# Second-layer softmax without its normalising pass: reciprocal row sums carried as rows through DRAM into the head outputs

## The chip, the cores and the metric

The kernel runs on one core of one Trainium2 chip. The metric is device microseconds of that core for one execution of the whole program; less is better. The core has TensorE (PE in the profile; its weight loads are listed apart as PEld), VectorE (DVE), ScalarE (ACT), GpSimd (POOL) and SyncE (SP), which here issues nearly all DMAs. On-chip memory is SBUF (128 partitions); TensorE writes into PSUM banks.

## The reference, cut to what matters

Two transformer-like layers work on 512 latent and 256 context tokens of width 1024. Layer 0 mixes by differential attention, layer 1 by grouped-query attention: 8 query heads of 128, two key/value heads, keys and values over all 768 tokens. In the last layer only the 512 latent tokens are queries. The change lies in layer 1:

```python
s = jnp.einsum('bqhgd,bkhd->bhgqk', qblk.astype(jnp.float32), k32) * scale
p = jax.nn.softmax(s, axis=-1)
return jnp.einsum('bhgqk,bkhd->bqhgd', p.astype(v.dtype), v)
...
def attend(qq, kk, vv, gate):
    o = sweep_attention(qq, kk, vv)
    o = o.reshape(o.shape[0], o.shape[1], BRANCH_WIDTH)
    return (o * jax.nn.silu(gate)) @ w_out
...
x = x + gate * rms_norm(y, post_g[i])
```

A softmax row is exp(s - max) divided by its sum. The division is linear in the row, so it can be done on the probabilities (768 numbers for each query and head) or on the head's output (128 numbers).

## The kernel before

**Precision.** Each large product is done with operands split into a high and a low part (`hi`, `lo`, type fp32r): three matmuls stand for one (`mm3`, `pv_mm`). So a weight that comes in as `raw` is copied by ACT into `whi`, and the remainder is taken into `wlo` by POOL or DVE.

**One head of layer 1.** Tokens are worked in four blocks of 128 queries (`m` = 0 to 3); two blocks make a pair (`ch` = 0, 1), so there are 8 x 2 = 16 pairs. For one block, `s1_units` does this: PE computes the scores of 128 queries by 768 keys into a two-bank PSUM tile (`sc`); DVE finds the negated row maximum; ACT takes the exponential into one half of an SBUF tile `pp` and sums each row into a small tile `l`; DVE inverts the sum; POOL multiplies the block by it in place (`scaled`, with `EN1 = 'p'`). After the second block of the pair, `turn` transposes the whole `pp` (128 x 1536) on DVE in blocks of 32 x 32, stores it to DRAM (`dr<-pp`, 768 KB) and loads it back in four pieces (`at<-dr`, 192 KB each), so that keys lie on the partitions. Two `pp` tiles and two `at` tiles are in turn.

`pv1_steps` then works on the pair in three steps of 256 keys: ACT copies a piece of `at` into `ah`, DVE takes the remainder into `al`, and PE multiplies both by the values into a bank of 256 columns. The output is transposed: features on partitions, the 256 queries of the pair along the row. ACT copies it into the head's tile `gT1[h]` (`g` in the profile). When both pairs of a head are done and its gate `sz` (SiLU of a projection) is there, POOL multiplies the head by the gate (`gate_mul1`); for the last head DVE does it half by half (`last_half`). All heads are split once more (`h<-g`) and enter the output projection, whose first quarter runs over seven heads while the last head is unfinished.

Beside this, PE has the projections of q and of the gate z to do, which a generator queue hands out as filling work. The q projection is followed by its norm (ACT `jk`, POOL `qrs`), the rotary products (DVE `ta`, `tb`) and their sum (POOL `q`).

**Layer 0** has the same shape, with two softmaxes a head; its normalisation is not touched. During layer 0, twelve 1 MB tiles of the conditioning weights are loaded (`araw<-in_ada_g`) and multiplied on PE (`bk<-araw,s`).

**What sets the order.** The program is written twice: a first pass (`Plan`) records every instruction with what it must wait for; `price` gives each an estimated cost, `schedule` lists them by engine queue with a model of hand-over times, DMA landing and the slowing of DVE and POOL by each other (`op.kind`), and `shift` moves the sort keys of some groups of instructions at random, one seed of `MOVES` after the other. The queues' order that comes out is then fixed for all five engines. So a changed instruction, a changed price or a changed list of seeds can re-sort every queue, in layer 0 too. DRAM scratch tiles are handed out in a ring (`dram`), six of them (`DRB`).

The prices for DMAs, by size in bytes, as (bytes per ns, base ns):

```python
rate, base = {196608: (207, 1450), 786432: (420, 900), 131072: (350, 2500)}.get(op.cost, (350, 1450))
```

Of the kernel before, what the change touches and what calls it, by code (L numbers as in the profile page):

```python
# [9 lines left out]
F32 = mybir.dt.float32  # L10
F32R = mybir.dt.float32r
AF = mybir.ActivationFunctionType
ALU = mybir.AluOpType
# [3 lines left out]
P = 128  # L17
# [60 lines left out]
QTR = 2.0  # L78
EG0 = 'v'
EP0 = 'p'  # L80
EN1 = 'p'
ESW = 'v'
EG1 = 'a'
LM = (4.5, 4.5)
AB = 2
P0B = 2
# [1 line left out]
PPB = 2  # L88
DRSPLIT = 1
DRB = 6  # L90
PEWAY = ((), ())


def f32(ap):
# [29 lines left out]
SLACK = 0  # L124


# [15 lines left out]
def free_size(ap):  # L142
    n = 1
    for d in ap.shape[1:]:
        n *= d
    return n


class Plan:


    def __init__(self, mem, psum, drams, sizes):
        self.mem, self.drams, self.sizes, self.turns = mem, drams, sizes, 0
        self.psum = dict(psum)
        self.banks = {t.tensor.name: t.free_size() for t in psum.values()}
        self.width = mem.shape[1]
        self.ops, self.offs, self.tail, self.seen = [], [0], None, {}
        self.marks = []
        self.pools, self.stack = [], {"left": [], "right": []}
        for q in QUEUE:  # L160
            setattr(self, q, Queue(self.add, QUEUE[q]))
# [3 lines left out]
        return Pool(self, name, side, psum)  # L165

    def scratch(self):
        self.tile = lambda *args, **kw: self.dram()
        return nullcontext(self)

    def dram(self):
        self.turns += 1
        return self.drams[(self.turns - 1) % len(self.drams)]


    @contextmanager
# [39 lines left out]
    def add(self, q, meth, args, kw):  # L216
        op = Op()
        op.n, op.eng, op.meth, op.args, op.kw = len(self.ops), q, meth, args, kw
        op.prio = op.n - self.offs[-1]
        op.next, op.head = None, op  # L220
        self.ops.append(op)
        if self.sizes is None:
            return op
        aps = [a for a in args if isinstance(a, bass.AP)]
        outs, ins = aps[:1], aps[1:]
        for k, v in kw.items():
            if isinstance(v, bass.AP):
                (outs if k in ("out", "accum_out") else ins).append(v)
        op.preds, op.soft = set(), set()
        fresh = []  # L230
        for aps_, w in ((ins, 0), (outs, 1)):
            for ap in aps_:
                far = ap.space == bass.MemoryType.DRAM
                if far and all(ap.tensor.name != d.tensor.name for d in self.drams):
                    continue
                name, spans, parts = (ap.tensor.name, [(0, 2048)], 1) if far else self.places(ap)
                if name not in self.banks and not far:
                    at = spans[0][0]
                    p = next(p for p in self.pools if p.open and p.base <= at < p.base + p.size)
                    p.users.add(op)  # L240
                    if p.mark is not None:
                        op.preds.add(p.mark)
                    held = p.held[max(lo for lo in p.held if lo <= at)]
                    ring = held[0]
                    held[2].add(op)
                    op.preds |= held[3]
                    if held[1] is None:
                        held[1] = len(ring)
                        ring.append(op)
                    if held[1] and ring[held[1] - 1] is not op:  # L250
                        op.soft.add(ring[held[1] - 1])
                if w and q == "PE":
                    spans = [(0, self.banks[name] * 4)]
                for lo, hi in spans:
                    for pg in self.pages(name, lo, hi):
                        keep = []
                        for h in self.seen.get((name, pg), ()):
                            hop, hlo, hhi, hp, hw = h
                            meet = hlo < hi and lo < hhi and hp & parts
                            if hop is not op and ((w or hw) and meet or name in self.banks and hop.eng != q):  # L260
                                op.preds.add(hop)
                            elif hop is not op and name in self.banks:
                                op.soft.add(hop)
                            if meet and w and (lo <= hlo and hi >= hhi or name not in self.banks and lo <= max(hlo, pg * 2048) and hi >= min(hhi, pg * 2048 + 2048)) and not hp & ~parts:
                                continue
                            keep.append(h)
                        self.seen[name, pg] = keep
                    fresh.append((name, lo, hi, parts, w))
        for name, lo, hi, parts, w in fresh:
            for pg in self.pages(name, lo, hi):  # L270
                self.seen.setdefault((name, pg), []).append((op, lo, hi, parts, w))
        self.price(op, outs, ins)
        if self.tail is not None:
            op.head = self.tail.head
            self.tail.next = op
            op.soft.add(self.tail)
            op.head.preds |= {p for p in op.preds if p.head is not op.head}
            op.head.soft |= {p for p in op.soft if p.head is not op.head}
        return op
# [11 lines left out]
    def price(self, op, outs, ins):  # L291
# [47 lines left out]
                op.cost = 190 + 2.155 * n  # L339
        if q in ("DVE", "POOL") and op.kind is None and op.meth not in ("reciprocal", "tensor_reduce", "memset"):  # L340
            if not any(ps) and outs[0].tensor.name not in self.banks:
                op.kind = 0.75 if n <= 8 else 0.5 if sum(free_size(a) > 8 for a in ins) >= 2 else 0.25


    def schedule(self, rank):
# [15 lines left out]
        while len(order) < count:  # L361
# [28 lines left out]
            elif op.kind == "D":  # L390
                s = max(s, land.pop(0))
                go = s + (450 if op.cost == 131072 else 480 if op.cost == 196608 else 440)
                rate, base = {196608: (207, 1450), 786432: (420, 900), 131072: (350, 2500)}.get(op.cost, (350, 1450))
                dma = max(dma, go + 300) + op.cost / rate
                end = dma + base - 300 + DPAD
                land.append(end)
# [199 lines left out]
def tile_backbone(  # L596
# [33 lines left out]
    drp = ctx.enter_context(pl.scratch())  # L630

    def small(n=1):
        return sm.tile([P, 8], F32, tag="sm", name=nm("sm"), bufs=24)[:, :n]

    banks = [ps1.tile([P, 512], F32, tag=f"bk{i}", name=f"bk{i}", bufs=1) for i in range(4)]
    scs = [ps1.tile([P, 2, 512], F32, tag=f"sc{i}", name=f"sc{i}", bufs=1) for i in range(2)]
# [43 lines left out]
    def turn(pool, pp, w=384):  # L680
        flat = pp.rearrange("p b u x -> p (b u x)")
        nc.vector.transpose(flat, flat)
        at = pool.tile([P, 4, w], F32, tag=f"at{w}", name=nm("at"), bufs=ATB if w == 384 else 1)
        for lo in range(0, 4, 4 // DRSPLIT):
            n = 4 // DRSPLIT
            dr = drp.tile([P // DRSPLIT, 4 * 384], F32, tag="dr", name=nm("dr"), bufs=DRB)[:, :4 * w]
            nc.sync.dma_start(dr, flat[32 * lo:32 * (lo + n), :])
            for a in range(4):
                nc.sync.dma_start(
                    at[32 * a:32 * a + 32, lo:lo + n, :],  # L690
                    dr.rearrange("(q j) (a c) -> a j q c", j=32, c=w)[a])
        return at

    def dma_way(layer, h, ch):
        return (h, ch) not in PEWAY[layer]
# [1221 lines left out]
    with pl.pool("t1", "right") as t1p:  # L1917
        gT1 = [None] * KT
        ropeb = con.tile([P, 2, 512], F32, tag="rope", name="ropeb")
        nc.scalar.dma_start(ropeb, rope_b)  # L1920
        gq = t1p.tile([P, 2, P], F32, name="gq")
        nc.scalar.dma_start(gq, b_qk_g.partition_broadcast(P))
        cosb = ropeb[:, 0, :].rearrange("p (t d) -> p t d", t=4)
        sinb = ropeb[:, 1, :].rearrange("p (t d) -> p t d", t=4)
# [19 lines left out]
        def head_rstd(o, isk=True):  # L1944
            ssq = small(2)
            for j in range(2):
                jk = t1p.tile([P, P], F32, tag="jk", name=nm("jk"), bufs=1)
                nc.scalar.activation(jk, o[:, j * P:(j + 1) * P], AF.Square, accum_out=ssq[:, j:j + 1])
            r = t1p.tile([P, 2], F32, tag="qrs", name=nm("qrs"), bufs=16)
            if isk:  # L1950
# [106 lines left out]
        def z1_proj(h):  # L2057
# [13 lines left out]
            szt1[h] = sz  # L2071
            gate_mul1(h)

        def s1_units(h, ms):
            res, pair = [], {}
            moved = dma_way(1, h, ms[0] // 2)

            def unit(m):
# [20 lines left out]
                else:  # L2099
                    pt = unit_row(pair[0], m % 2)  # L2100
                    pv_, src = pt.rearrange("p (j n) -> p j n", j=2), scv
                l = small()
                nc.scalar.activation(pv_, src, AF.Exp, scale=sr, bias=nmx, accum_out=l)
                nc.vector.reciprocal(l, l)
                scaled(EN1, pt, pt, l)
                if not moved:
                    res.append(pt)
                elif m % 2:
                    res.append(turn(t1q, pair[0]))

            return res, [Step(lambda m=m: unit(m), 0.97) for m in ms]

        def pv1_steps(h, at, ch, after, ts, ms):
# [19 lines left out]
            def mstep(kt):  # L2133
# [6 lines left out]
                if kt == 4:  # L2140
                    if ch == 0:
                        gT1[h] = t1p.tile([P, 512], F32, tag="g1", name=nm("g1"), bufs=8)
                    (nc.scalar.copy if EG1 == "a" else nc.vector.tensor_copy)(*heads_out(gT1[h][:, ch * 256:ch * 256 + 256], o, moved))
                    close(o)
                    if ch == 1 and h < KT - 1:
                        done1.add(h)
# [234 lines left out]
```

## Time and profile before

| | |
|---|---|
| time, median of 3 runs | 755.72 us (755.34 to 755.8) |
| profiled execution, its own time | 757.93 us |
| its span, first to last instruction | 755.8 us |
| mean granted TensorE clock | 0.996 |
| DMA moved | 131.75 MB, mean 174 GB/s |

The span in 40 equal slices, in tenths of busy time (the last line is the granted clock):

```profile
PE   7999999999999999899999999999999989999996
PEld 6788888888878898797989998899999988888986
DVE  4445899988988869787889844789547787799744
ACT  6544477767676646666569853784476776678741
POOL 5463787885795738747755412467779887674201
PEclk9999999999999999999999999999999999999999
```

One slice is 18.9 us. Layer 0 runs to about 500 us, the projections of layer 1 follow, its attention lies between about 550 and 700 us, and the output projection runs to the end. In rows of groups and tiles, `a<-b,c` means that an instruction writes tile a from b and c; then come the shape, the count, the busy time and the mean of one, and the idle time of the engine just ahead of it with what ended it. In rows of order in time, the first two numbers are the start and the duration in us, and the bracket is the idle time ahead of the instruction and who ended it. A line of waits reads: who waited, on whom, us in total, times, longest.

### The profile page before, as it was taken

To read this page: it belongs to the slowest core of one execution; us is meant where nothing else is said; L and a number is where in the kernel's file an instruction comes from. 1 tells how busy PE (TensorE), PEld (TensorE's weight loads), DVE (VectorE), ACT (ScalarE), POOL (GpSimd) and SP (SyncE) were. 2 spreads that over 40 slices of the span, in tenths; PEclk is the share of its full clock that TensorE was granted. 3 is DMA by queue.
4 is the path that set the end of the run, shared out by engine and by line. 5 is a ranking of instruction groups with operands and counts; after the bars stand their busy time and mean duration, and the time that the engine had idled before them with its cause. 6 is when DMAs were issued, how large, how long until landed. Compare 5 with 4: busy or idle time off the path is not lost. (4 is left out here: it accounts for less than half of the span.)

```text
span 755.8 us, 13984 instructions
## 1 busy us (share of the span) xinstructions
PE 733.9 (97%) x5046; PEld 654.3 (87%) x5046; DVE 567.1 (75%) x881; ACT 480.0 (64%) x1085; POOL 466.7 (62%) x512
## 2 busy tenths in 40 slices
PE   7999999999999999899999999999999989999996
PEld 6788888888878898797989998899999988888986
DVE  4445899988988869787889844789547787799744
ACT  6544477767676646666569853784476776678741
POOL 5463787885795738747755412467779887674201
PEclk9999999999999999999999999999999999999999
DMA  9933263647474655835666182034436785888613
GB/s 347 405 123 124 95 198 109 188 164 223 140 221 142 212 165 176 255 100 172 229 171 179 31 307 84 2 97 157 145 117 190 224 257 163 232 239 266 165 46 111
DMA packets 51444, 131.75 MB, mean 174 GB/s; under 512 B 6448, under 2 KB 27184, under 8 KB 49840
## 3 DMA queue, kind: packets, MB, share of 16 engines
q1 hardware_dynamic: 47952, 125.73, 52.7%
q10 hardware_dynamic: 3424, 5.15, 2.1%
q8 instruction: 39, 0.64, 0.4%
q14 instruction: 29, 0.24, 0.1%
HBM read 97.56 MB, written 29.10 MB: 168 GB/s over the span
## 5 line engine op out<-in xcount | busy, mean ns | idle before, releaser
L509 PE MATMUL bk<-whi,h 128*128 128x256 f32 (+1 forms) x1184 | 244.0, 298 | 2.9 <-DVE tb L509 1.8
L509 PE MATMUL bk<-h,whi 128*128 128x512 f32 (+2 forms) x832 | 222.4, 348 | 0.1
L509 POOL TENSOR_TENSOR wlo<-raw,whi 128x256 fp32r<-128x256 f32 x200 | 171.1, 879 | 56.1 <-ACT whi L509 53.7
L509 PEld LDWEIGHTS bk<-whi,h 128*128 128x128 f32 x1184 | 189.6, 189 | 13.9 <-issue 2.9
L509 PE MATMUL bk<-wlo,h 128*128 128x256 f32 (+1 forms) x592 | 172.3, 298 | 0.0
L509 PEld LDWEIGHTS bk<-h,whi 128*128 128x128 f32 x832 | 144.4, 188 | 15.6 <-issue 2.8
L509 PE MATMUL bk<-h,wlo 128*128 128x512 f32 (+2 forms) x416 | 144.0, 348 | 0.0
L509 POOL TENSOR_SCALAR pp<-pp,sm 128x768 f32<-128x768 f32 (+1 forms) x78 | 82.0, 1054 | 68.0 <-DVE sm L509 58.4
L509 PEld LDWEIGHTS bk<-wlo,h 128*128 128x128 f32 x592 | 109.8, 188 | 4.9 <-issue 1.6
L509 DVE TENSOR_REDUCE sm<-sc 128x1 f32<-128x768 f32 (+2 forms) x114 | 101.0, 893 | 14.7 <-PE sc L509 14.5
L509 DVE TENSOR_TENSOR al<-at,ah 128x512 fp32r<-128x512 f32 x103 | 98.7, 978 | 13.7 <-ACT ah L509 9.9
L509 ACT CAST whi<-raw 128x1024 fp32r<-128x1024 f32 (+1 forms) x70 | 71.5, 1023 | 27.1 <-PE bk L509 14.9
L509 PEld LDWEIGHTS bk<-h,wlo 128*128 128x128 f32 x416 | 78.3, 188 | 8.7 <-issue 2.4
L509 ACT CAST ah<-at 128x512 fp32r<-128x512 f32 x103 | 61.7, 618 | 33.3 <-PE bk L509 21.0
L509 DVE STREAM_TRANSPOSE pp<-pp 128x1536 f32<-128x1536 f32 (+1 forms) x39 | 61.4, 1577 | 5.7 <-POOL pp L509 5.6
L509 DVE SCALAR_TENSOR_TENSOR pp<-p,sm,pp 128x768 f32<-128x768 f32 (+1 forms) x46 | 55.8, 1219 | 4.4 <-POOL pp L509 2.8
L509 PE MATMUL sc<-qk,qk 64*128 64x384 f32 (+1 forms) x480 | 50.7, 341 | 0.4 <-DVE qk L509 0.4
L509 ACT ACTIVATE jk<-bk 128x128 f32<-128x128 f32 (+4 forms) x66 | 22.7, 345 | 41.8 <-PE bk L509 22.8
L509 ACT ACTIVATE pp<-sc,sm 128x768 f32<-128x768 f32 (+1 forms) x46 | 35.4, 770 | 21.5 <-DVE sm L509 20.8
L509 PEld LDWEIGHTS sc<-qk,qk 64*128 64x128 f32 x480 | 38.3, 184 | 10.7 <-issue 3.5
L509 POOL TENSOR_TENSOR sz<-sz,za 128x384 f32<-128x384 f32 (+1 forms) x24 | 28.3, 1180 | 23.8 <-ACT za L509 23.8
L509 ACT ACTIVATE za<-za 128x384 f32<-128x384 f32 (+1 forms) x72 | 40.0, 559 | 4.7 <-DVE za L509 4.1
(206 smaller groups left out, 1365.1 us busy)
## 6 DMA issues: line engine op xcount, KB each, us to landing
dr<-pp SPq DMA_DIRECT2D x32, 768.0 KB, 4.0
at<-dr SPq DMA_DIRECT2D x128, 192.0 KB, 4.3
raw<-in_a_w SPq DMA_DIRECT2D x30, 512.0 KB, 3.9
araw<-in_ada_g SPq DMA_DIRECT2D x12, 1024.0 KB, 7.0
raw<-in_b_w SPq DMA_DIRECT2D x20, 512.0 KB, 3.8
ag<-in_ada_s SPq DMA_DIRECT2D x16, 512.0 KB, 9.9
raw<-in_w_out SPq DMA_DIRECT2D x16, 512.0 KB, 4.5
sw<-qr ACTq DMA_DIRECT2D x32, 128.0 KB, 2.1
```

Of the source, the lines that this page charges most:

```text
L509: self.ops.append(getattr(eng, meth)(*args, **kw))
```

## The change

The probabilities of layer 1 stay unnormalised. The row sums of a pair are collected in columns 0 and 32 of a 128 x 64 tile `lt`; after the pair's transpose they are inverted by DVE (128 x 2), `spread` transposes `lt` on DVE in blocks of 32 x 32, so that four partitions hold all 256 reciprocals, stores these as one row to a DRAM scratch (`rw`, a ring of four) and loads the row into all 128 partitions of a tile `rl` (128 x 256, a ring of two that begins in the place of the tile `gq`). When the pair's output is done, ACT copies it as before and POOL multiplies it by `rl`; for the last head, DVE does both in one instruction that reads PSUM.

The planner changes with it: scratch tiles are kept in two rings and their stores in order, the price of 128 KB and 1 MB DMAs and the slowing of one-operand POOL instructions by DVE are set anew, the ring of small tiles shrinks from 24 to 22, a junk tile `jk` becomes bf16, and 84 seeds are added to `MOVES` behind the 200 that are there.

```diff
@@ planner
+RWB = 4
@@ MOVES
-    303396361, ... 207578973)
+    303396361, ... 207578973,
+    1064440296, ... 63380170)
@@ Plan.add
+                if far and w:
+                    if name[:2] in self.stores:
+                        op.soft.add(self.stores[name[:2]])
+                    self.stores[name[:2]] = op
@@ Plan.price
-                op.kind = 0.75 if n <= 8 else 0.5 if sum(free_size(a) > 8 for a in ins) >= 2 else 0.25
+                op.kind = 0.75 if n <= 8 else 0.5 if sum(free_size(a) > 8 for a in ins) >= 2 else 0.6 if q == "POOL" else 0.25
@@ Plan.schedule
-                rate, base = {196608: (207, 1450), 786432: (420, 900), 131072: (350, 2500)}.get(op.cost, (350, 1450))
+                rate, base = {196608: (207, 1450), 786432: (420, 900), 131072: (350, 1500), 1048576: (300, 2400)}.get(op.cost, (350, 1450))
@@ tile_backbone
-        return sm.tile([P, 8], F32, tag="sm", name=nm("sm"), bufs=24)[:, :n]
+        return sm.tile([P, 8], F32, tag="sm", name=nm("sm"), bufs=22)[:, :n]
...
+    def spread(dst, lt):
+        n = 4 * lt.shape[-1]
+        nc.vector.transpose(lt, lt)
+        rw = drp.tile([1, T], F32, tag="rw", name=nm("rw"), bufs=RWB)[0, :n]
+        nc.sync.dma_start(rw.rearrange("(b x) -> b x", b=4), lt[0:P:32, :])
+        nc.sync.dma_start(dst, rw.partition_broadcast(P))
...
-        gq = t1p.tile([P, 2, P], F32, name="gq")
+        gq = t1p.tile([P, 2, P], F32, tag="gq", name="gq", bufs=2)
...
-                jk = t1p.tile([P, P], F32, tag="jk", name=nm("jk"), bufs=1)
+                jk = t1p.tile([P, P], BF, tag="jk", name=nm("jk"), bufs=1)
...
+        rls = {}
+        lts = [t1q.tile([P, 64], F32, name=f"lt{i}", bufs=1) for i in range(2)]
+        for lt in lts:
+            nc.gpsimd.memset(lt, 1.0)
@@ s1_units
-                l = small()
-                nc.scalar.activation(pv_, src, AF.Exp, scale=sr, bias=nmx, accum_out=l)
-                nc.vector.reciprocal(l, l)
-                scaled(EN1, pt, pt, l)
+                if m % 2 == 0:
+                    lts.append(lts.pop(0))
+                    pair[1] = lts[-1]
+                l = pair[1].rearrange("p (u x) -> p u x", x=32)[:, :, 0]
+                nc.scalar.activation(pv_, src, AF.Exp, scale=sr, bias=nmx, accum_out=l[:, m % 2:m % 2 + 1])
                 if not moved:
                     res.append(pt)
                 elif m % 2:
                     res.append(turn(t1q, pair[0]))
+                if m % 2:
+                    nc.vector.reciprocal(l, l)
+                    rls[h, m // 2] = t1p.tile([P, 256], F32, tag="gq", name=nm("rl"), bufs=2)
+                    spread(rls[h, m // 2], pair[1])
@@ pv1_steps
-                    (nc.scalar.copy if EG1 == "a" else nc.vector.tensor_copy)(*heads_out(gT1[h][:, ch * 256:ch * 256 + 256], o, moved))
+                    gs, rl = gT1[h][:, ch * 256:ch * 256 + 256], rls.pop((h, ch))
+                    if h < KT - 1:
+                        nc.scalar.copy(*heads_out(gs, o, moved))
+                        to, by = heads_out(gs, rl, moved)
+                        nc.gpsimd.tensor_tensor(to, to, by, ALU.mult)
+                    else:
+                        nc.vector.tensor_tensor(*heads_out(gs, o, moved), heads_out(gs, rl, moved)[1], ALU.mult)
```

More of the change, by code (lines that the diff above doesn't have):

```diff
@@ L80 @@
 EP0 = 'p'
-EN1 = 'p'
 ESW = 'v'
-EG1 = 'a'
 LM = (4.5, 4.5)
@@ L149, with __init__ @@
 class Plan:
-    def __init__(self, mem, psum, drams, sizes):
-        self.mem, self.drams, self.sizes, self.turns = mem, drams, sizes, 0
+    def __init__(self, mem, psum, scratches, sizes):
+        self.mem, self.sizes = mem, sizes
+        self.scratches = {tag: list(ring) for tag, ring in scratches.items()}
+        self.stores = {}
+        self.drams = {t.tensor.name for ring in scratches.values() for t in ring}
         self.psum = dict(psum)
@@ L167, in scratch, with dram @@
     def scratch(self):
-        self.tile = lambda *args, **kw: self.dram()
+        self.tile = lambda *args, **kw: self.dram(kw["tag"])
         return nullcontext(self)
-    def dram(self):
-        self.turns += 1
-        return self.drams[(self.turns - 1) % len(self.drams)]
+    def dram(self, tag):
+        ring = self.scratches[tag]
+        ring.append(ring.pop(0))
+        return ring[-1]
     @contextmanager
@@ L233, in add @@
                 far = ap.space == bass.MemoryType.DRAM
-                if far and all(ap.tensor.name != d.tensor.name for d in self.drams):
+                if far and ap.tensor.name not in self.drams:
                     continue
                 name, spans, parts = (ap.tensor.name, [(0, 2048)], 1) if far else self.places(ap)
+                if far and w:
+                    if name[:2] in self.stores:
+                        op.soft.add(self.stores[name[:2]])
+                    self.stores[name[:2]] = op
                 if name not in self.banks and not far:
@@ L2367 @@
             mem = mp.tile([P, MEM // 4], F32, name="mem")[:]
-            drams = [drp.tile([P // DRSPLIT, 4 * 384], F32, name=f"dr{i}")[:, :] for i in range(DRB)]
+            scratches = {
+                "dr": [drp.tile([P // DRSPLIT, 4 * 384], F32, name=f"dr{i}")[:, :] for i in range(DRB)],
+                "rw": [drp.tile([1, T], F32, name=f"rw{i}")[:, :] for i in range(RWB)],
+            }
             sizes, pl = None, None
             while pl is None or sizes != pl.sizes:
-                pl = Plan(mem, psum, drams, sizes)
+                pl = Plan(mem, psum, scratches, sizes)
                 tile_backbone(pl, *args)
```

12 rows, old and new, of the table MOVES are left out of this document.

## The prediction

> **What bounds the kernel now.** I read the page's busy line first, then tables of busy time by stretch, then what TensorE (PE) waited for, and last the order of time around those waits.
>
> ```profile
> PE 733.9 (97%) x5046; PEld 654.3 (87%) x5046; DVE 567.1 (75%) x881; ACT 480.0 (64%) x1085; POOL 466.7 (62%) x512
> 130.00:400.00 270.00, 265.82 (x1885) 231.28 (x1884) 227.58 (x325) 176.33 (x376) 190.83 (x177) 1.00 0.59 181
> 545.00:605.00 60.00, 60.00 (x411) 56.95 (x410) 39.52 (x72) 42.40 (x107) 51.94 (x71) 1.00 0.59 178
> 605.00:640.00 35.00, 31.12 (x212) 29.42 (x211) 27.49 (x44) 24.49 (x59) 27.93 (x29) 0.95 0.74 223
> 640.00:700.00 60.00, 57.62 (x331) 50.87 (x330) 52.76 (x67) 46.19 (x97) 36.53 (x34) 1.00 0.81 236
> 700.00:749.00 49.00, 49.00 (x325) 44.78 (x324) 27.24 (x41) 22.98 (x52) 9.92 (x18) 1.00 0.30 88
> ```
>
> The columns of the stretches are: from:to, length, busy PE, PEld (weight loads), DVE, ACT, POOL, granted clock, DMA share, GB/s. PE is the bound, and the change touches none of its instructions. A gain can come only from time in which PE stands still or runs slowly. The changed layer's attention lies in 545 to 700. Its first 60 us and the 49 us after it hold no PE idle time. The 95 us between hold 3.88 + 2.38 = 6.26 us. That is most of what this change can reach directly. What ended those waits, over the whole run:
>
> ```profile
> PE bk L509 <- DMA araw<-in_ada_g: 3.6, 2, 1.9
> PE bk L509 <- DVE al L509: 1.8, 3, 0.8
> PE bk L509 <- DVE tb L509: 1.8, 1, 1.8
> PE bk L509 <- ACT ah L509: 1.2, 1, 1.2
> PE bk L509 <- ACT g L509: 0.9, 2, 0.5
> PE sc L509 <- ACT pp L509: 0.9, 2, 0.6
> ```
>
> **The normalising step: taken out.** Thirty-two POOL scalings go. In their place come 14 POOL products (128x256; the last head's two move to DVE).
>
> ```profile
> L509 POOL TENSOR_SCALAR pp<-pp,sm 128x768 f32<-128x768 f32 x32 | 38.1, 1192 | 26.4 <-DVE sm L509 16.9 <-ACT h L509 7.1 <-ACT za L509 1.6
> L509 POOL TENSOR_TENSOR q<-ta,tb 128x256 f32<-128x256 f32 x13 | 10.1, 778 | 1.8 <-DVE tb L509 1.6
> L509 DVE RECIPROCAL sm<-sm 128x2 f32<-128x2 f32 x14 | 2.0, 151 | 0.0
> L509 DVE STREAM_TRANSPOSE pp<-pp 128x1536 f32<-128x1536 f32 x32 | 56.6, 1769 | 5.6 <-POOL pp L509 5.6
> L509 DVE STREAM_TRANSPOSE arow<-arow 128x512 f32<-128x512 f32 x4 | 2.8, 703 | 0.0
> ```
>
> POOL: 38.1 us less, 14 x 0.78 = 10.9 more: 27 us free. DVE: 32 reciprocals of 0.15 become 16 (-2.4); 16 transposes of 128x64 come in. Their price on the line through 1769 ns (1536 wide) and 703 ns (512 wide) is 703 - 448 x 1.04 = 237 ns, so +3.8; two products take the place of two ACT copies, and I price them like such a copy (0.37 us, quoted below with the last pair; +0.7). DVE +2.1 us in 155, its cover being the 7 us in which it is idle in 640 to 700. The two memsets, the smaller rings and the narrower junk tile cost nothing on PE's path: POOL's idle time covers the memsets.
>
> What counts is not the 27 us but the wait: the 1.77 us DVE transpose of a pair stands behind two POOL scalings, and everything on DVE stands behind the transpose.
>
> ```profile
> 617.19 1.88 POOL L509 TENSOR_SCALAR pp<-pp,sm 128x768 f32<-128x768 f32 x1
> 619.10 1.78 DVE L509 STREAM_TRANSPOSE pp<-pp 128x1536 f32<-128x1536 f32 x1 [0.74 <-POOL pp L509]
> 620.80 1.46 DVE L509 TENSOR_TENSOR al<-at,ah 128x512 fp32r<-128x512 f32 x1
> 622.31 0.50 PE L509 MATMUL bk<-al,vh 128*128 128x256 f32 x2 [0.84 <-DVE al L509]
> 623.27 0.39 PE L509 MATMUL bk<-whi,h 128*128 128x256 f32 x1 [0.46 <-ACT g L509]
> 627.58 1.78 DVE L509 STREAM_TRANSPOSE pp<-pp 128x1536 f32<-128x1536 f32 x1 [0.73 <-POOL pp L509]
> 630.84 0.42 DVE L509 TENSOR_TENSOR ta<-bk,ropeb 128x256 f32<-128x256 f32 x1 [0.63 <-ACT jk L509]
> 631.80 0.36 PE L509 MATMUL bk<-whi,h 128*128 128x256 f32 x1 [1.80 <-DVE tb L509]
> 655.25 1.14 ACT L509 CAST ah<-at 128x512 fp32r<-128x512 f32 x2 [1.57 <-DMA at<-dr]
> ```
>
> POOL's scaling ends at 619.07, DVE has idled 0.74 for it, "al" ends at 622.26 and PE starts at 622.31. Without the scaling that gap of 0.84 goes, and the 0.46 behind it, whose ACT copy follows the same matmuls: 1.3 us. The two waits for "pp" (0.9) are a score bank whose exponential waits for a free probability buffer; a buffer leaves a scaling earlier, so they go. The "ah" wait (1.2) is a load whose store stood behind the same scaling; it goes. Of "tb" (1.8) only the 0.73 that the transpose waited comes off: DVE next waits for ACT "jk", which ends where it did. Taken: 1.3 + 0.9 + 1.2 + 0.7 = 4.1. Ends: 0 (every gap is held by the next wait) and 6.26. I stand nearer the upper end because three of four chains run through the removed row.
>
> **The clock.**
>
> ```profile
> 620.00:623.40 3.40, 2.10 (x15) 1.69 (x14) 3.40 (x5) 1.28 (x6) 2.62 (x3) 1.00 1.00 277
> 629.80:633.20 3.40, 1.60 (x12) 1.43 (x11) 2.77 (x8) 3.27 (x11) 3.04 (x6) 1.00 0.58 234
> 633.20:636.60 3.40, 3.40 (x17) 3.40 (x16) 1.79 (x4) 2.41 (x8) 2.02 (x2) 0.50 0.80 194
> ```
>
> After a stretch with 1.60 of 3.40 us busy the clock stood at 0.50 for 3.4 us; after one with 2.10 it did not fall. Half speed over 3.4 us costs 1.7. With 0.73 more busy the stretch has 2.33, above 2.10, so I take 1.7 off. Ends: another halving (+1.7), and 1.7 off. [...]
>
> **The row's way through DRAM.** Each pair adds two DMAs on SP (4 partitions out, 128 KB in).
>
> ```profile
> dr<-pp SPq DMA_DIRECT2D x32, 768.0 KB, 4.0
> at<-dr SPq DMA_DIRECT2D x128, 192.0 KB, 4.3
> sw<-qr ACTq DMA_DIRECT2D x32, 128.0 KB, 2.1
> DMA to landing us min/median/max: 2.8/4.1/7.4
> 706.33 0.34 SPq L509 DMA_DIRECT2D dr<-pp  x1
> 721.18 0.37 ACT L509 COPY g<-bk 128x256 f32<-128x256 f32 x1
> 698.18 1.74 SPq L509 DMA_DIRECT2D at<-dr  x4
> 706.32 0.60 ACT L509 CAST ah<-at 128x512 fp32r<-128x512 f32 x1
> ```
>
> The third line's 128 KB and the second line's landing give 2.1 to 4.3 us for each of the two; I take 2.1 + 4.3 = 6.4 us for both, at worst two of the longest landing of "dr" and "at" in this layer (7.4), 14.8. For the last pair 14.9 us lie between its store (706.33) and the copy that will need the row (721.18): hidden at both ends. On SP it is 32 issues of 0.34 us, 11 us over 155 in a queue that mostly stands waiting; the bytes are 16 x 129 KB, 2.1 MB beside 36 MB. In front of the gate product stands one more POOL product (0.78); behind it only the final split of the head waits, while PE is full (49.00 of 49.00). Cost 0; if the cover is gone, up to the slow rival below.
>
> **The plan's prices.** The order of every queue is computed by the planner, and the diff changes three prices and 84 seeds, so all queues are re-sorted. A 1 MB load lands in the plan 1240 + 1048576/350 + 1450 ns = 5.7 us after its issue before the change (1240 being 440 for the issue and 800 of padding), 1240 + 1048576/300 + 2400 ns = 7.1 us after it.
>
> ```profile
> DMA to landing us min/median/max: 5.1/7.0/10.0
> 225.60 1.07 PE L509 MATMUL bk<-araw,s 128*32 128x512 f32 x8 [1.70 <-DMA araw<-in_ada_g]
> 319.78 1.07 PE L509 MATMUL bk<-araw,s 128*32 128x512 f32 x8 [1.91 <-DMA araw<-in_ada_g]
> ```
>
> "araw" lands in 7.0 (median), so the old plan was 1.3 early; with 1.45 more in the plan, the two waits of the first layer shrink by 1.45 each: 2.9 off (ends 0 and 3.6). Against that stand waits that the new order brings. No row shows them; I bound them by 0 and by the whole 4.1 taken off above, and take 2.0, as much as is left of the 6.1 listed in that layer.
>
> **Sum.** -4.1 - 1.7 - 2.9 + 2.0 = -6.7. The profiled execution took 757.93 (its span 755.8), 2.2 above the median of 755.72. 757.93 - 6.7 = 751.2 for such an execution, 749.0 as a median.
>
> **Rivals.**
>
> Waits change hands: DVE is busy 52.76 of 60 us in 640 to 700 and gets 2.1 us more, so PE's waits move from POOL's result to DVE's queue. For: the 1.80 gap ends in a DVE instruction that next waits for ACT. Against: DVE idled for POOL in both chains above. The 4.1 and 1.7 do not come, 2.9 and 2.0 stay: -0.9, 754.8.
>
> The first layer gains too: in 130 to 400 PE is busy 265.82 but loads weights for 231.28, so 38.7 of 270 us pass without one although PE looks full; a re-sorting that closes a tenth of it gives 3.9 more than the sum: 745.1. For: seeds and prices reach that layer's queues. Against: nothing of its work changes. [...]
>
> SP stands at the broadcast: it cannot be issued before its row has landed, and the four "at" loads of the pair may be queued behind it. Then they start 4.0 (a store's landing) + 0.34 later. One pair has 706.32 - 699.92 - 4.2 = 2.2 us to spare, the one at 655.25 has none: 2.1 late at least. Four such pairs of 16 eat the 6.7; from there on the kernel is slower, at five (10.5) by 3.8: 759.5. For: SP's queue runs in order. Against: the store of the row is small and can go out beside the big one, whose landing the loads wait for anyway.
>
> **How the numbers follow.** Forecast 0.54 (746 to 752.5), first layer too 0.18, waits change hands 0.18, SP 0.10. This kernel's measurement tells about 0.2% (1.5 us) from no change. Faster: 0.54 + 0.18 + a fifth of the third case, 0.76; same 0.13, the bulk of it; slower: SP and a rest, 0.11. The range leaves out SP (0.10) and the lower half of the first layer's case: 743.5 to 755.8, holding 0.8.
>
> **What would show it.** Right: no DVE transpose of the second layer waits for POOL; POOL some 27 us less busy; PE idle in the attention of layer two near 4 us (2.0 left + 2.0 new), no halved clock there; "araw" waits under 1 us in total. Wrong: PE waits for "ah" with SP standing at the row's landing; the clock halved again; PE busy time itself changed by several us, which would mean that the order, not the removed step, made the difference.

## The result, and the profile after

The changed kernel takes 788.74 us (median of 4 runs, 787.26 to 789.66) against 755.53 us (752.75 to 755.8) before: 1.0446 times the time, 95% interval 1.0417 to 1.0476. It is 33 us slower; the forecast was 749.0, with 743.5 to 755.8 as its range.

The profiled execution took 788.62 us with a span of 786.8, so 31.0 us of span are to be found. The busy line of the page, then the tables by stretch (columns as in the prediction):

```profile
PE 744.9 (95%) x5046; PEld 661.1 (84%) x5046; DVE 564.6 (72%) x883; ACT 479.9 (61%) x1083; POOL 443.7 (56%) x496
130.00:400.00 270.00, 267.82 (x1889) 232.00 (x1887) 223.88 (x327) 176.89 (x379) 200.45 (x184) 1.00 0.58 183
545.00:605.00 60.00, 57.78 (x397) 54.41 (x396) 40.45 (x76) 37.41 (x100) 42.20 (x63) 1.00 0.59 177
605.00:640.00 35.00, 28.16 (x177) 26.64 (x177) 20.81 (x29) 22.14 (x48) 14.79 (x17) 0.90 0.69 200
640.00:700.00 60.00, 48.08 (x261) 41.58 (x262) 40.27 (x58) 34.81 (x80) 27.84 (x32) 0.94 0.58 176
700.00:749.00 49.00, 42.58 (x257) 38.72 (x256) 36.46 (x48) 32.87 (x64) 13.84 (x11) 0.94 0.66 189
```

The first layer is as it was: in 130 to 400 PE does 1889 matmuls where it did 1885. From 605 to 700 every engine does less in each stretch; in 700 to 749, where before only the last of the attention and the output projection were left, the attention is still going on. PE is idle for 6.8, 11.9 and 6.4 us of the three stretches from 605 on, where it was idle for 3.9, 2.4 and 0, and its clock is down in all three. In the whole run it is busy for 744.9 us with the same 5046 matmuls that took 733.9. No engine is full there; they wait for each other.

A handy measure is the stage from the first exponential of layer 1 to the end of the span. The rows of the probability tiles give the start (type and count, ns min/median/max, first and last start); before, then after:

```profile
L509 ACT ACTIVATE pp<-sc,sm,qrs x32: 979/994/1008, 556.3 to 694.4; 128x768 f32<-128x768 f32 x32
```

```profile
L526 ACT ACTIVATE pp<-sc,sm,qrs x32: 977/992/1017, 559.0 to 716.2; 128x768 f32<-128x768 f32 x32
```

755.8 - 556.3 = 199.5 us before, 786.8 - 559.0 = 227.8 after: 28.3 of the 31.0 us are lost in this stage, 2.7 before it.

What PE waited for in 545 to 760, then what SP waited for in 560 to 760 (us in total, times, longest):

```profile
PE sc L526 <- ACT pp L526: 13.3, 5, 4.1
PE bk L526 <- ACT ah L526: 12.1, 7, 4.5
```

```profile
SPq L526 <- POOL g L526: 57.1, 11, 7.9
...
SPq L526 <- DMA rw<-lt: 5.4, 4, 2.4
```

PE waits for exponentials and for copies of `at`, both ACT's. The longest waits of all are SP's: 57.1 us for POOL `g`, the product with the reciprocals. Before, SP waits 0.4 us for POOL `g`, once. The wait for the row's landing (`rw<-lt`), which the slow rival was priced by, is a tenth of it.

Order in time shows how one turns into the other. SP, POOL, ACT, DVE and PE of the changed kernel between 582 and 611 us (start, duration; in brackets the idle time before and who ended it):

```profile
594.04 0.34 SPq L526 DMA_DIRECT2D rl<-rw  x1
...
597.10 0.45 SPq L526 DMA_DIRECT2D raw<-in_b_w  x1
598.97 1.81 SPq L526 DMA_DIRECT2D at<-dr  x4
609.42 0.34 SPq L526 DMA_DIRECT2D rl<-rw  x1
609.85 0.38 SPq L526 DMA_DIRECT2D dr<-pp  x1
```

```profile
589.33 3.99 POOL L526 TENSOR_TENSOR wlo<-raw,whi 128x256 fp32r<-128x256 f32 x5
593.28 0.74 POOL L526 TENSOR_TENSOR g<-g,rl 128x256 f32<-128x256 f32 x1
605.90 2.80 POOL L526 TENSOR_TENSOR wlo<-raw,whi 128x256 fp32r<-128x256 f32 x4 [11.89 <-ACT whi L526]
608.65 0.74 POOL L526 TENSOR_TENSOR g<-g,rl 128x256 f32<-128x256 f32 x1
```

```profile
582.77 0.37 ACT L526 COPY g<-bk 128x256 f32<-128x256 f32 x1 [0.65 <-PE bk L526]
...
604.78 1.04 ACT L526 CAST whi<-raw 128x1024 fp32r<-128x1024 f32 x1 [4.31 <-DMA raw<-in_b_w]
605.73 0.99 ACT L526 ACTIVATE pp<-sc,sm,qrs 128x768 f32<-128x768 f32 x1
```

```profile
599.83 1.77 DVE L526 STREAM_TRANSPOSE pp<-pp 128x1536 f32<-128x1536 f32 x1
```

```profile
606.86 0.54 PE L526 MATMUL sc<-kh,qh 128*128 128x384 f32 x1 [4.08 <-ACT pp L526]
```

`rl` is a ring of two tiles. A broadcast overwrites the tile of the pair two back, so it must wait until POOL has multiplied by that one. The rows at 594.04 and 609.42 are the broadcasts of pairs 3 and 4. On SP each stands directly behind the four `at` loads of its own pair (598.97 are pair 4's) and ahead of the stores and loads of the pairs that follow. Product 1 ends at 594.02 and SP issues broadcast 3 at 594.04; product 2 ends at 609.39 and broadcast 4 goes out at 609.42. Before each of them SP stands, and with it all that is queued behind.

The first product is late because POOL has other work ahead of it: ACT's copy was done at 583.14, and POOL is at rotary sums, norms and weight remainders until 593.28. From there on the delay feeds itself. A weight load (`raw`) that stood behind broadcast 3 goes out only at 597.10; ACT then waits for it 4.31 us, and the exponential that is queued behind that weight's copy starts at 605.73, for which PE has waited 4.08 us. POOL has waited 11.89 us for the same weight with product 2 queued behind it, whose copy ACT had made at 592.80; that product is late, so the next broadcast is late. Pair 5, which DVE had transposed by 601.60, is stored at 609.85, 8.2 us later, although nothing of it depends on the broadcast. The late product makes the loads late, and the late loads make the next product late: a loop, turned once a pair. Ring slots are freed only by products, so broadcasts 3 to 16 leave at the products' pace, from 594.04 to 734.5: 10.8 us a pair. Eleven of these 14 go out within 0.03 us of the end of the product two pairs back.

### The profile page after: what moved, and what is told of

Same layout as the page of the kernel before. It is cut to its first block, busy times and chain, and to the rows that moved or that the text cites. A ratio compares the mean times of both kernels' runs of the same rounds, so it can differ in the third digit from the quotient of the medians.

```text
span 786.8 us, 14021 instructions
## 1 busy us (share of the span) xinstructions
PE 744.9 (95%) x5046; PEld 661.1 (84%) x5046; DVE 564.6 (72%) x883; ACT 479.9 (61%) x1083; POOL 443.7 (56%) x496
## 4 chain that ended last, share of the span: by engine, by line
PE 70%; DMA 10%; DVE 6%; ACT 5%; issue 4%; POOL 3%; SPq 2%; ACTq 0%; DVEq 0%; POOLq 0%
PE bk L526 58%; PE sc L526 12%; DMA dr<-pp 4%; DMA at<-dr 3%; DVE al L526 2%; SPq L526 2%; ACT pp L526 1%; DVE pp L526 1%; POOL wlo L526 1%; DMA raw<-in_b_w 1%; DMA rw<-lt 1%; ACT ah L526 1%; DVE sm L526 1%; DMA xt<-in_x 1%; POOL g L526 1%
## 5 line engine op out<-in xcount | busy, mean ns | idle before, releaser
L526 PE MATMUL bk<-h,whi 128*128 128x512 f32 (+2 forms) x832 | 227.4, 353 | 2.0 <-DVE gate L526 2.0
L526 POOL TENSOR_TENSOR wlo<-raw,whi 128x256 fp32r<-128x256 f32 x200 | 168.5, 867 | 84.8 <-ACT whi L526 75.6
L526 PE MATMUL bk<-wlo,h 128*128 128x256 f32 (+1 forms) x592 | 170.4, 298 | 0.0
L526 PEld LDWEIGHTS bk<-h,whi 128*128 128x128 f32 x832 | 146.5, 190 | 18.3 <-issue 3.6
L526 DVE TENSOR_TENSOR al<-at,ah 128x512 fp32r<-128x512 f32 x103 | 100.3, 988 | 37.9 <-ACT ah L526 33.0
L526 POOL TENSOR_SCALAR pp<-pp,sm 128x768 f32<-128x768 f32 (+1 forms) x46 | 44.6, 973 | 37.4 <-DVE sm L526 37.3
L526 ACT ACTIVATE jk<-bk 128x128 bf16<-128x128 f32 (+4 forms) x66 | 22.7, 344 | 40.3 <-PE bk L526 23.4
```

The source lines that it names most:

```text
L526: self.ops.append(getattr(eng, meth)(*args, **kw))
```

## The experiments

Three theories. One: SP, whose DMAs go out in its queue's order (pair 5's store above, ready at 601.60, went out at 609.85 behind broadcast 4), stands at the broadcast for the product two pairs back, and the loop above sets the pace. Two: the re-sorted plan (prices and seeds) is to blame. Three: the added DMAs themselves cost the time. The first set is to take the wait away in two ways and does the planner's part alone.

**The plan alone.** The kernel before with the new prices, the new `kind` and the 84 seeds, nothing else (excerpts of the edits, here and below):

```diff
+    1064440296, ... 63380170)
+ ... else 0.6 if q == "POOL" else 0.25
-    131072: (350, 2500)}
+    131072: (350, 1500), 1048576: (300, 2400)}
```

> The kernel before with the planner's part of the change alone: the new prices of 128 KB and 1 MB DMAs, the new slowing of one-operand POOL instructions, and the 84 added seeds; no instruction changed. Theories 1 and 3: within 745 to 762 (the prediction's term for the first layer alone would give 752.6). Theory 2: 775 or more.

Measured: 756.94 us (753.63 to 760.65), ratio 1.0016 (0.9994 to 1.0038). Stage from the first exponential 755.7 - 556.2 = 199.5 us, as before. The second theory falls as far as prices and seeds go. The second scratch ring and the order of the stores, which this run leaves out, are in all the runs that follow.

**No row.** The reciprocals don't travel; each head is multiplied by a constant tile of ones, so the output is not normalised:

```diff
-                    rls[h, m // 2] = t1p.tile([P, 256], F32, tag="gq", name=nm("rl"), bufs=2)
-                    spread(rls[h, m // 2], pair[1])
+                    rls[h, m // 2] = rl1
...
```

> Leaves out the row's way: the reciprocals are not transposed, stored or broadcast, and the heads are multiplied by one constant tile of ones; so the probabilities stay unnormalised and the output is not normalised. Theory 1: no broadcast, no wait, 745 to 755 (this is what taking the scaling out of the chain is worth by itself; my prediction's terms give 749). Theory 2: still 775 or more. Theory 3: 745 to 755 as theory 1; e1 tells these two apart.

Measured: 749.19 us (747.14 to 751.77), ratio 0.9923 (0.9893 to 0.9953); stage 750.0 - 555.9 = 194.1 us. With the POOL products still there and the row gone, the whole loss is gone, and what the forecast promised is there. The loss lies in the row's way: in its wait or in its DMAs.

**A prompt product.** All heads are multiplied by DVE straight out of PSUM, as the last head is, so that the product cannot lie behind POOL's weight remainders:

```diff
-                    if h < KT - 1:
+                    if False:
```

> All heads are multiplied as the last one is: DVE reads PSUM and the row and writes the head (no ACT copy, no POOL product); the ring stays at two. Theory 1: the product no longer waits in POOL's queue (it came 8 to 16 us after the copy), the row tile is free at once; SP's wait for the product under 15 us; time 750 to 762. If the ring of two is too short even with a prompt product: 765 to 780. Theories 2 and 3: 780 to 790.

Measured: 802.67 us (800.91 to 804.42), ratio 1.0629 (1.0599 to 1.066); stage 802.4 - 554.9 = 247.5 us. The first theory had expected a gain here, and missed. SP's list, then DVE, SP and ACT in order of time:

```profile
SPq L526 <- DVE g L526: 50.3, 12, 8.0
```

```profile
598.97 0.39 DVE L526 TENSOR_TENSOR g<-bk,rl 128x256 f32<-128x256 f32 x1
...
609.35 0.73 DVE L526 TENSOR_TENSOR al<-at,ah 128x512 fp32r<-128x512 f32 x1 [2.34 <-ACT ah L526]
...
612.85 0.38 DVE L526 TENSOR_TENSOR g<-bk,rl 128x256 f32<-128x256 f32 x1
```

```profile
599.38 0.34 SPq L526 DMA_DIRECT2D rl<-rw  x1
599.77 0.90 SPq L526 DMA_DIRECT2D at<-dr  x2
...
613.26 0.34 SPq L526 DMA_DIRECT2D rl<-rw  x1
```

```profile
605.07 1.14 ACT L526 CAST ah<-at 128x512 fp32r<-128x512 f32 x2 [4.21 <-DMA at<-dr]
```

The product did not become prompt. PE ends pair 3's multiplications at 595.79 and DVE takes their product at 612.85, 17 us later; over the 16 pairs the median of this delay is 12.8 us, and in the changed kernel it is 10.9. The wait has changed its owner, and the loop is closed through DVE's queue instead of POOL's. Product 2 ends at 599.36 and broadcast 4 goes out at 599.38. Behind it, at 599.77, go the last two `at` loads of pair 4. ACT waits for them until 605.07, DVE waits for ACT, and product 3 stands in DVE's queue behind pair 4's last `al` (609.35). It ends at 613.23, and broadcast 5 goes out at 613.26. So this run shows that moving the product to DVE does not help; what a prompt product would do, it can't say. Why the plan puts the product there was not looked into.

**The row without the wait.** The second set keeps every DMA. First, the row goes its whole way and is not used: the product takes a constant tile, so nobody waits for the ring and the output is not normalised; the `qt` ring (tiles for the rotated q and k) is 9 instead of 10, to make room for the constant:

```diff
-                    gs, rl = gT1[h][:, ch * 256:ch * 256 + 256], rls.pop((h, ch))
+                    gs, rl = gT1[h][:, ch * 256:ch * 256 + 256], rl1
...
```

> Keeps the row's whole way (reciprocal, transpose, store, broadcast into the ring of two) and the POOL products, but multiplies by a constant tile of ones, so that nobody reads the row tiles and no broadcast waits for a product; the output is not normalised. One q tile fewer makes room for the constant. Theory 1 (SP stands at the broadcast until the product two pairs back): 746 to 757. Theory 3 (the 32 added DMAs and the DVE work by themselves): 780 or more.

Measured: 764.05 us (763.45 to 768.05), ratio 1.0127 (1.01 to 1.0154), more than expected. But the stage takes 762.5 - 565.0 = 197.5 us, 30 less than in the changed kernel: all 32 DMAs are there and the loss of the stage is not. The third theory falls: the stage is 3.4 us longer than without the row (194.1), not 34. What is left of the loss lies ahead of the first exponential (565.0 against 556.3) and comes back below.

**A longer ring.** Four tiles (and `qt` 8), then three (and `qt` 9). A first version with four tiles and `qt` at 10 gave no time: one of its pools needs 54.66 KB of each partition where 52.66 are left, so `qt` gives up the room.

```diff
-                    rls[h, m // 2] = t1p.tile([P, 256], F32, tag="gq", name=nm("rl"), bufs=2)
+                    rls[h, m // 2] = t1p.tile([P, 256], F32, tag="gq", name=nm("rl"), bufs=4)
...
```

> Four row tiles instead of two; two q tiles fewer (8 instead of 10) make room. Theory 1: SP's wait for POOL g near zero, 746 to 758. A theory that two pairs more in flight are not enough, because products come 8 to 16 us late in POOL's queue whatever the ring: 765 to 785. Theory 3: 785 or more.

> Three row tiles, one q tile fewer. Theory 1 as a loop (product of pair k, broadcast of pair k+ring, loads behind it, product of pair k+ring): the loop's length is shared by three pairs instead of two; measured 11 us a pair at two against 9 needed, so 7 to 8 at three: no longer the bound, 747 to 762. If it is not a loop but a fixed delay for every broadcast: half way, 765 to 775.

Four tiles: 751.75 us (749.58 to 758.04, 10 runs), ratio 0.996 (0.9936 to 0.9983), stage 750.9 - 554.5 = 196.4. In SP's list POOL `g` has 0.8 us left of 57.1. Three tiles: 766.33 us (763.06 to 771.27), ratio 1.0152 (1.0107 to 1.0196), stage 769.5 - 570.9 = 198.6. In the stage three tiles do nearly what four do, and SP no longer waits for POOL `g` at all. The whole run falls into the range that had been named for a fixed delay of every broadcast (765 to 775), but for what happened before the stage.

**A later broadcast.** The ring stays at two, `qt` at 10. `spread` only stores the row; the broadcast is planned when the pair's first copy of `at` is done, so on SP it comes not directly behind its own pair's loads, as in the changed kernel, but behind the store of the next pair as well:

```diff
+                if kt == 0:
+                    first = pl.ops[-2]
+                    rl = t1p.tile([P, 256], F32, tag="gq", name=nm("rl"), bufs=2)
+                    bc = nc.sync.dma_start(rl, rls[h, ch].partition_broadcast(P))
+                    if isinstance(pl, Plan) and pl.sizes is not None:
+                        bc.soft.add(first)
+                    rls[h, ch] = rl
...
```

> Ring of two kept. The broadcast is planned only after the pair's first ACT copy of its transposed probabilities, so that on SP it stands behind the loads of its own pair and the stores of later ones. Theory 1: the wait on SP shrinks to under 10 us, 747 to 760. If it is the row tile's ring itself, wherever the broadcast stands: 775 to 790.

Measured: 751.11 us (748.03 to 751.97), ratio 0.9931 (0.9907 to 0.9955). SP's waits and order, then the stretches of the attention:

```profile
SPq L526 <- POOL g L526: 1.3, 2, 0.8
```

```profile
614.86 1.74 SPq L526 DMA_DIRECT2D at<-dr  x4
616.65 0.43 SPq L526 DMA_DIRECT2D dr<-pp  x1
...
621.22 0.32 SPq L526 DMA_DIRECT2D dr<-pp  x1
621.59 0.42 SPq L526 DMA_DIRECT2D rl<-rw  x1
```

```profile
545.00:605.00 60.00, 58.90 (x406) 55.46 (x405) 40.17 (x73) 40.72 (x99) 43.66 (x64) 1.00 0.66 189
605.00:640.00 35.00, 33.63 (x247) 32.69 (x246) 29.83 (x47) 28.83 (x71) 24.42 (x30) 1.00 0.86 258
640.00:700.00 60.00, 59.38 (x347) 52.60 (x346) 53.77 (x76) 47.61 (x98) 22.31 (x25) 1.00 0.86 259
```

```profile
L526 ACT ACTIVATE pp<-sc,sm,qrs x32: 978/992/1002, 557.4 to 686.5; 128x768 f32<-128x768 f32 x32
```

Here pair 6's loads go out at 614.86, the stores of pairs 7 and 8 at 616.65 and 621.22, and only then broadcast 6. The stage takes 750.2 - 557.4 = 192.8 us, 35.0 less than in the changed kernel and 6.7 less than before, with the same ring, the same products and the same DMAs. Only the place of the broadcast on SP differs, and with it the order that the planner makes: the products now start 0.9 us (median) after the multiplications. PE does 247 matmuls in 605 to 640 where the changed kernel does 177, and the clock stays at 1.00. This version beats both kernels, the one before by 0.7%.

**Controls.** Because four tiles came with a shorter `qt` ring, the third set runs the changed kernel with `qt` at 8 and nothing else, the late broadcast with `qt` at 9, and the late broadcast with four tiles and `qt` at 8:

```diff
-            kn = t1p.tile([P, 256], F32, tag="qt", name=nm("kn"), bufs=10)
+            kn = t1p.tile([P, 256], F32, tag="qt", name=nm("kn"), bufs=8)
...
```

> The changed kernel (ring of two row tiles) with 8 q tiles instead of 10, as in e6 but without its longer ring. If e6 won by the ring: 780 to 795, with SP waiting about 50 us for POOL g. If it won by the smaller q ring and the re-sorted order that follows from it: 750 to 758.

> e8 (late broadcast, ring of two) with 9 q tiles instead of 10. e5 and e7, the two runs with 9 q tiles, were late before the attention began (first exponential at 565.0 and 570.9 us against 556.3 in the kernel before). If the 9 q tiles do that, by re-sorting the whole plan: first exponential at 563 or later, time 757 to 768. If e5 and e7 were late for the row itself: 749 to 754 with the first exponential near 557.

> Both repairs together: four row tiles, 8 q tiles, late broadcast. Theory 1: the wait is gone with either, so together they add nothing: 748 to 753. If the wait was only halved by each: 742 to 747.

The changed kernel with `qt` 8: 801.32 us (797.39 to 803.42), ratio 1.0605 (1.056 to 1.0649); above the expected 780 to 795; stage 798.3 - 566.7 = 231.6 us, and SP stands again:

```profile
SPq L526 <- POOL g L526: 56.0, 10, 9.2
```

So it was the ring of `rl`, not that of `qt`, that made four tiles fast. The late broadcast with `qt` 9: 761.6 us (761.43 to 762.1), ratio 1.0086 (1.0051 to 1.012), stage 759.9 - 565.5 = 194.4. Both repairs together: 764.16 us (763.24 to 764.95), ratio 1.0118 (1.0089 to 1.0148), stage 763.1 - 566.8 = 196.3; 748 to 753 had been expected for it, and missed. The two repairs do not add up in the stage either (192.8 and 196.4 alone), as there is but one wait to take away.

Five kernels (no wait, three tiles, and these three) start their exponentials at 565 to 571 us, all others at 554 to 559. The time is lost before the attention. The late broadcast with `qt` 9, then four tiles, from 0 to 545:

```profile
0.00:545.00 545.00, 532.79 (x3714) 464.95 (x3715) 407.83 (x647) 339.49 (x760) 336.91 (x351) 1.00 0.52 170
```

```profile
0.00:545.00 545.00, 537.77 (x3786) 473.51 (x3787) 412.34 (x656) 344.51 (x774) 345.92 (x367) 1.00 0.52 172
```

By 545 us the five have done 3686 to 3716 matmuls and all the others 3764 to 3786, with no part of the change near: another order of the same work. It comes with all three kernels that have `qt` at 9 and with two of the three that have it at 8, and with none that has 10, so the shorter `qt` ring is the suspect, and not the row. Why one kernel with `qt` 8 escapes it stays open. For the question at hand the stage decides: 227.8 and 231.6 us with the broadcast directly behind its own pair's loads and a ring of two (247.5 with DVE's products), 192.8 to 198.6 in the seven kernels that have no such wait, 199.5 without the change.

One thing stays open. In the three kernels where SP stands, the product starts 10.9 to 12.8 us (median) after its pair's multiplications; in the seven where it does not, 0.8 to 1.2. The late product is part of the loop, but no run has the ring of two, the broadcast directly behind its own loads, and a prompt product that reads the row, all together. The run without the wait lets one estimate it: with its products at 1.1 us, 12 of its 14 later broadcasts go out after the product two pairs back has ended, the other two 0.7 and 3.8 us before. By that a prompt product would leave SP little to wait for, even with two tiles.

Putting the broadcast on ACT's or POOL's own queue was not tried.

## Why the prediction was wrong

**The step that failed** is "The row's way through DRAM", priced "Cost 0" and "hidden at both ends". It counted how long a row takes from its store to its use (6.4 us, at worst 14.8, against 14.9 of room) and asked only whether the row comes in time. It did: no product of the changed kernel waited for its row, and the broadcasts landed soon after their issue:

```profile
DMA to landing us min/median/max: 2.9/3.8/5.4
```

It never asked when the broadcast may begin. The `rl` tiles are a ring of two, stated in the diff, so each broadcast has a second condition, the product two pairs back, and SP, whose queue was named as one that "mostly stands waiting", stands there with other pairs' stores and loads behind it. The term of 0 measured 28.3 + 6.7 = 35 us: the changed kernel's stage against that of the late broadcast.

**The slow rival** (0.10) came nearest: SP stands at the broadcast, and PE waits for `ah`. But it had the cause, the victims and the price wrong. The cause was to be the landing of the row's store (5.4 us of waits in all) and not the ring. The pair's own loads were to stand behind the broadcast; they stand ahead of it, and the next pairs' stores and loads are behind. And the price was a delay of 4.3 us, 2.1 of them felt, in five of 16 pairs, not a loop whose delay feeds itself. Hence 759.5 and not 789. Its "Against" argued that the row's store is small; SP's 57.1 us of waits were for a free tile and had nothing to do with a size.

**The scaling out of the chain (-4.1) and the clock (-1.7)** were right in kind, once the wait is gone; the size is open. In the late broadcast PE is idle 1.1 + 1.4 + 0.6 = 3.1 us in 545 to 700 (forecast: near 4), no clock is halved (1.00 in all three stretches), and the stage is 6.7 us shorter than before (forecast for these two: 5.8). But over the seven kernels without the wait the stage is shorter by 0.9 to 6.7 us, and five of them still have a halving while PE is at work (a clock of 0.95 to 0.98 in the stretches that hold it).

**The first layer's terms (-2.9 and +2.0)** are refuted as a gain. The waits for `araw` went as foreseen with the new price (3.6 us before, none listed with the plan alone), but the plan alone gained nothing (1.0016): other small waits came in their place (ACT `qr` 1.4 and ACT `p` 1.2 us, ACT `h` 1.1 for 0.2). That the late broadcast lands at 751.11 and no row at 749.19, beside a forecast of 749.0, is therefore half luck: the attention of the late broadcast gave what the two layers together were to give, the first layer nothing. "The first layer gains too" (0.18) failed as well: in the changed kernel PE does 1889 matmuls for 1885 in 130 to 400, and loads weights for 232.0 us for 231.3. The 38.7 of 270 us without a weight load that it started from, 14%, were no more than the two stretches from 605 to 700 had (16 and 15%).

**Waits change hands** (0.18) failed: in the late broadcast DVE is busier than before in 640 to 700 (53.77 for 52.76) and PE waits less.

**The small prices** held, by the groups of the changed kernel in 545 to 750:

```profile
L526 POOL TENSOR_TENSOR g<-g,rl 128x256 f32<-128x256 f32 x14 | 13.5, 966 | 2.4 <-ACT g L526 2.4
L526 DVE STREAM_TRANSPOSE lt<-lt 128x64 f32<-128x64 f32 x16 | 3.8, 235 | 0.1
```

The transpose was priced 237 ns on a line through two wider ones and took 235. POOL is 23.0 us less busy (466.7 to 443.7) for the 27 forecast; the products cost 966 ns and not 780. Beside 33 us all of this is small.

**What would show it wrong** had been named: PE waiting for `ah` with SP at the row's landing, the clock halved again, and PE busy time changed by several us. The clock was halved, and PE waited for `ah` with SP at the broadcast, though for a free tile and not for a landing. PE busy time grew by 11.0 us with the same matmuls; the prediction would have read that as the work of the order, but some 8 us of it are the halved clock (last section). PE waits twelve times for `pp` and `ah`, up to 4.5 us, and with two more `rl` tiles 2.5 us of those 25.4 are left. But the late broadcast is as fast without one more buffer.

## What to carry to other kernels

For every DMA that is put in, ask for both its conditions: is its source ready, and is its destination free. With a ring of n tiles the second is the last reader of the tile n turns back, and if that reader itself, or what stands ahead of it in its engine's queue, depends on a transfer queued behind the DMA, the loop sets the pace of the stage however small the transfer is (here 10.8 us a pair, for 128 KB). Two cures worked here: to issue it later, behind the next turn's store as well, which takes no memory, or to lengthen the ring. Judge such a trial by its stage, as a re-sorted plan moved the start of the stage by some 10 us here (554 to 559 against 565 to 571).

## What the runs showed of the hardware

The clock. The six halvings of the changed kernel between 605 and 749 begin at 607.06, 627.54, 651.43, 675.33, 699.22 and 740.18 us, whole multiples of 3.41 us apart, and each lasts 3.41. Stretches of that length, cut on this grid:

```profile
603.65:607.06 3.41, 0.20 (x1) 0.20 (x2) 0.20 (x2) 2.25 (x5) 1.16 (x2) 1.00 0.83 179
607.06:610.47 3.41, 3.41 (x10) 3.08 (x10) 1.36 (x2) 2.48 (x5) 3.33 (x5) 0.50 0.04 8
...
668.50:671.91 3.41, 1.56 (x11) 1.24 (x9) 0.64 (x2) 0.75 (x3) 0.00 (x0) 1.00 0.95 253
671.91:675.33 3.42, 0.97 (x3) 0.49 (x3) 3.42 (x5) 0.89 (x1) 0.00 (x0) 1.00 0.38 160
675.33:678.74 3.41, 3.17 (x8) 2.69 (x9) 1.49 (x5) 3.09 (x8) 0.00 (x0) 0.50 0.96 234
```

The six stretches ahead of the halvings hold 0.20, 0.80, 1.20, 0.97, 0.38 and 0.14 us of matmuls. Of the others from 603.65 on, the emptiest, 1.56, 1.79 and 2.09, were followed by one at a clock of 1.00. In the trace of before, a stretch with 1.60 of 3.40 us stood ahead of a halving and one with 2.10 did not. No sharp line between the two shows in these rows. If the halving at 607.06 is put down to the wait of 4.08 us that ended at 606.86, that wait cost some 1.7 us more than its own length, an estimate from half of 3.41. From 605 to 749 the clock takes 0.10 x 35 + 0.06 x 60 + 0.06 x 49 = 10.0 us off PE in the changed kernel, 0.05 x 35 = 1.8 before, and nothing to 700 in the late broadcast. Of the 28.3 us some 8 are clock by this estimate, the rest waits.
